# A hybrid attention, convolution and gated-MLP layer: weight sums of four pairs of the up-projection on GpSimd, and another order of the q, k, v chunks

## The chip, the cores and the metric

The kernel runs on one core of a Trainium2 chip. The time is that of the device in microseconds for one execution; a kernel's time is the median of several runs. A core has a matrix engine (TensorE, PE in the profile; its weight loads are PEld), three engines for elementwise work, VectorE (DVE), ScalarE (ACT) and GpSimd (POOL), and SyncE (SP), whose queue issues most of the DMA transfers. Each engine works through its own list of instructions.

## The reference

One layer in float32 over 1024 latent tokens of width 1024 with 256 context tokens ahead of them; batch 1. Cut to what matters:

```python
h  = modulate(x, norm1_w, sh1, sc1)               # RMSNorm, scaled and shifted
q, k, v, hy, gates = split_proj(h @ w_in + b_in)  # q 1024, k 256, v 256 wide, ...
q = apply_rope(rmsnorm(q, q_norm_w)); k = apply_rope(rmsnorm(k, k_norm_w))
attn_o = attend(q, cat(kc, k), cat(vc, v))        # 8 heads of 128, 2 heads of k and v, 1280 keys
hy_o = hyena(hy, ...)                             # long convolution through FFTs
x = x + g1 * merge(attn_o, hy_o, gates, ...)
u = dwconv3(modulate(x, norm2_w, sh2, sc2) @ w_up + b_up, conv_w, conv_b)
a, g = split(u)                                   # 2816 columns each
x = x + g2 * ((gelu(a) * g) @ w_down + b_down)
out = rmsnorm(x, final_norm_w)
```

## The kernel before

Every float32 product is made of three matmuls (lines 184 to 186 issue them): each operand is split into a high part, a rounded copy that ACT casts, and a low part, the difference, that DVE or POOL subtracts (`whi` and `wlo` of a weight block, `PTh` and `PTl` of attention weights).

**q, k and v.** The last part of the projections (lines 996 to 1002) goes over six rounds. In each, one gate chunk (`gate_chunk`, two blocks of columns) is followed by one chunk of 256 columns of q, k or v (`qkv_chunk`): k, v, and four of q. A chunk is projected for eight groups of 128 tokens; what comes behind the matmuls (bias, norm, rotation, transposes, storing) is put on the list `steps` and drained in the following chunk, so that PE has other matmuls meanwhile. A chunk of v only gets its bias and is stored to `v_d`; those of k and q are rotated (`norm_rope`: `ropeA`, `ropeB` on DVE), transposed on PE (`transposed`, tile `tr`) and stored. Beside the first rounds runs the long convolution (`background`).

**Attention.** Sixteen items (loop over `n`), one head and 512 query rows each. For each of ten key blocks, four transposes bring the softmax's weights into a tile `tp` (two buffers), ACT casts `PTh`, DVE subtracts `PTl`, and three matmuls accumulate the output. Scores of the next item are put between. The output of an item is copied to `ou` by ACT, and finished in the next item at key block 7 (`finish`): the reciprocals of the softmax's denominators go out through HBM (`rd_d`) and come back on all partitions as `rb`, POOL multiplies `ou` by it, ACT casts the result (`oTh`), and POOL subtracts `oTl`.

**Sums for the down-projection.** POOL also forms, for eleven items, four sums of blocks of `w_down`: `weights_load` fetches four 256 KB blocks on SP's queue into two tiles `wd` at key block 1, `weight_sums` makes four 128x512 operations at block 7 and stores the results to `ws_d`. The first of them is pinned behind the last operation of `finish`, by `issue_after`, which sets only the order on an engine. Tiles `wd` come from the pool `sgp`, tag "sg" with three buffers.

**Up-projection.** 22 pairs of column blocks, each pair by a scheme of seven products for a 2x2 split. `fetch` loads blocks of `w_up`, `prepare` forms the sums of blocks that products 5, 6, 7 and 3 take (four DVE operations on `wsum` per pair), casts `whi` and returns the subtraction `wlo`. Products of later pairs are put ahead where there is one; in the last four pairs, from `j` = 18, products of the down-projection (8) come between.

The order on each engine is the result of a scheduler, which takes the traced program and its dependences; the code's order is only the start of it.

Of the kernel before, what the change touches and what calls it, by code (L numbers as in the profile page):

```python
# [8 lines left out]
F32 = mybir.dt.float32  # L9
# [6 lines left out]
P = 128  # L16
# [149 lines left out]
def build(tc, A, out, stop=99):  # L166
# [447 lines left out]
    def proj_tok(pool, w, cols, kind, ci, br, qkn, tabs, key0, tok0, nb, bgn=0):  # L614


        ps = pmm.tile([P, 4, 256], F32, name="mm", tag="mm")
        n = len(cols)
        steps = []
        for i, c in enumerate(cols):  # L620
            h, c = c // 512, c % 512
            for k in range(KT):
                mm3(ps[:, i], hTh[h][:, k, c:c + P], hTl[h][:, k, c:c + P], *w[k], k == 0, k == KT - 1)
            if bgn:
                background(bgn)

        def norm_rope(j):
            qr = pool.tile([P, 2, 2, P], F32, name="qr", tag="qr", bufs=nb)
            q3 = qr.rearrange("p t h d -> p t (h d)")
            tt(q3, ps[:, j:j + 2], br.unsqueeze(1).to_broadcast([P, 2, 256]), ALU.add)  # L630
            if kind == "v":
                kt = key0 // P + j
                st(out=v_d[:, kt:kt + 2], in_=q3)
                return None
            ss = stat.tile([P, 4], F32, name="ss", tag="ss4")
            A_ = pool.tile([P, 2, 2, P], F32, name="ropeA", tag="A", bufs=nb)
            for i in range(4):
                S.activation(out=A_[:, i // 2, i % 2], in_=qr[:, i // 2, i % 2], func=AF.Square,
                             accum_out=ss[:, i:i + 1])
            r = rsqrt(ss, 4, HD)  # L640
            q4 = qr.rearrange("p t h d -> p (t h) d")
            for i in range(4):
                S.activation(out=q4[:, i], in_=q4[:, i], func=AF.Copy, scale=r[:, i:i + 1])
            if kind == "kc":
                tt(A_.rearrange("p t h d -> p (t h) d"), q4, qkn[:, 0:1, :].to_broadcast([P, 4, P]), ALU.mult)
            else:
                t0 = tok0 // P + j
                B_ = pool.tile([P, 2, 2, P], F32, name="ropeB", tag="B")
                for o_, tb in ((A_, tabs[0]), (B_, tabs[1])):
                    tt(o_, qr, tb[:, t0:t0 + 2].unsqueeze(2).to_broadcast([P, 2, 2, P]), ALU.mult)  # L650
                sub(A_[..., 0:64], A_[..., 0:64], B_[..., 64:128])
                tt(A_[..., 64:128], A_[..., 64:128], B_[..., 0:64], ALU.add)
            return A_

        def transposed(j, A_):
            tp = ptr.tile([P, 2, 2, P], F32, name="tr", tag="tr")
            for t in range(2):
                for h in range(2):
                    T.transpose(tp[:, h, t], A_[:, t, h], ident)
            t3 = tp.rearrange("p h t d -> p h (t d)")  # L660
            sh = pool.tile([P, 2, 256], F32, name="sth", tag="sth", bufs=nb)
            S.copy(out=sh, in_=t3)
            if kind == "q":
                o = tok0 + j * P
                st(out=qT_d[ci - 2][:, :, o:o + 256].rearrange("h p t -> p h t"), in_=sh)
            else:
                o = key0 + j * P
                st(out=kT_d[:, :, o:o + 256].rearrange("h p t -> p h t"), in_=sh)

        hold = {}  # L670
        for j in range(0, n, 2):
            steps.append(lambda j=j: hold.__setitem__(j, norm_rope(j)))
            if kind != "v":
                steps.append(lambda j=j: transposed(j, hold[j]))
        return steps
# [290 lines left out]
    def gate_chunk(ci, behind=(0, 0)):  # L966
        w = load_w(A["w_in"][12 + ci])
        for m2 in range(2):
            m = 2 * ci + m2
            ps = proj_ch(w, m2, 2)  # L970
            for h in range(2):
                sg = sgpool[0].tile([P, 512], F32, name="sg", tag="sg", bufs=sgpool[1])
                S.activation(out=sg, in_=ps[:, 512 * h:512 * h + 512], func=AF.Identity, bias=bcol(12 + m))  # L973
                (ld if ci > 6 else st)(out=sg_d[m, :, 512 * h:512 * h + 512], in_=sg)
            drain()
            for _ in range(behind[m2]):
                item.score()
# [17 lines left out]

    background(4)
    tabs = rope_tables(1)
    for ci in range(6):
        gate_chunk(ci)
        if ci == 2:  # L1000
            tabs = rope_tables(0)
        qkv_chunk(ci, tabs)
    drain()
# [100 lines left out]

    KH = NJ // 2
    ws_d = tc.dram_tile([4, KH, P, 512], F32, name="ws_d")

    wds = []

    def weights_load(k):  # L1110

        wds[:] = [sgp.tile([P, 2, 512], F32, name="wd", tag="sg") for _ in range(2)]
        for i, (n_, k_) in enumerate(((0, k), (1, k), (1, KH + k), (0, KH + k))):
            ld(out=wds[i // 2][:, i % 2], in_=A["w_down"][n_, k_])

    def weight_sums(k, after):

        t1, t3, t2, t4 = (wds[i // 2][:, i % 2] for i in range(4))
        with tc.issue_after(after.ins):
            sub(t1, t3, t1, G)  # L1120
        sub(t3, t2, t3, G)
        sub(t2, t2, t1, G)
        sub(t4, t4, t2, G)
        for n_, t_ in enumerate((t1, t2, t3, t4)):
            ld(out=ws_d[n_, k], in_=t_)

    late = None
    for n in range(16):
        cur, g = item.Pt, item.h // 4
        nxt = None  # L1130
        if n < 15:
            if (n + 1) % 2 == 0:
                q = load_q((n + 1) // 2, sgp.tile([P, L], F32, name="qf", tag="th", bufs=2))
            nxt = Item(n + 1, q)
        o_ps = pO.tile([P, 512], F32, name="o", tag="o")
        pend = []

        def av(kt, th, tl):
            mm3(o_ps, vv[0][:, kt, g * P:g * P + P], vv[1][:, kt, g * P:g * P + P], th, tl, kt == 0, kt == 9)

        for kt in range(10):
            tp = pT.tile([P, 512], F32, name="tp", tag="tp")
            for i in range(4):
                T.transpose(tp[:, i * P:i * P + P], cur[i][:, kt * P:kt * P + P], ident)  # L1144
            th = ap2.tile([P, 512], F32R, name="PTh", tag="PTh", bufs=4)
            S.copy(out=th, in_=tp)  # L1146
            tl = ap2.tile([P, 512], F32R, name="PTl", tag="PTl", bufs=4)
            sub(tl, tp, th)
            pend.append((kt, th, tl))
            if len(pend) > 2:  # L1150
                av(*pend.pop(0))
            if kt in (1, 3, 5, 7) and nxt:
                nxt.score()
            if kt == 1 and 1 <= n <= KH:
                weights_load(n - 1)
            if kt == 7 and late:
                last_ = finish(*late)
                if n <= KH:
                    weight_sums(n - 1, last_)
        while pend:  # L1160
            av(*pend.pop(0))
        ou = ap2.tile([P, 512], F32, name="ou", tag="ou", bufs=2)
        S.copy(out=ou, in_=o_ps)
        late = (n, ou)
        item = nxt
        if n == 12:
            zts = [z_load(*i) for i in ZT[:3]]
            raw_hy = sgp.tile([P, 2, 2, 256], F32, name="raw_hy", tag="th", bufs=2)
            ld(out=raw_hy, in_=A["w_hy"][0].rearrange("i p (k c) -> p i k c", k=2))
# [295 lines left out]
    def fetch(p, j):  # L1465
        if p == 9 or p == 8 and j < 4:
            raws[p, j] = half_block(act_d[0, j]), half_block(A["w_down"][0, j])
        for b_ in {1: (A11,), 2: (A12,), 6: (A21, A22, A11), 3: (A12,)}.get(p, ()):
            raws[p, j, b_] = half_block(A["w_up"][j, b_])

    def prepare(p, j):
# [3 lines left out]
        if p >= 8:  # L1475
# [13 lines left out]
                for d, src in zip(parts_, r_):  # L1489
                    sub(d[1], src, d[0])  # L1490
            return lows
        if p == 6:
            r21, r22, r11 = (raws[6, j, b_] for b_ in (A21, A22, A11))
            s1, s2, s3 = new(), new(), new()
            tt(s1, r21, r22, ALU.add)
            sub(s2, s1, r11)
            sub(s3, r11, r21)
            sums_[j] = s1, s2, s3
            src = s2
        elif p == 7:  # L1500
            src = sums_[j][2]
        elif p == 5:
            src = sums_[j][0]
        elif p == 4:
            src = raws.pop((6, j, A22))
        elif p == 3:
            src = new()
            sub(src, raws.pop((3, j, A12)), sums_.pop(j)[1])
        else:
            src = raws.pop((p, j, A11 if p == 1 else A12))  # L1510
# [124 lines left out]
    n_ = 0  # L1635
# [238 lines left out]
```

## Time and profile before

| | |
|---|---|
| median of 3 runs | 2023.29 us (2020.77 to 2024.64) |
| profiled execution, its span, its mean granted clock | 2025.56 us, 2023.8 us, 0.975 |
| busy: PE, PEld, DVE, ACT, POOL | 94%, 78%, 76%, 48%, 21% |
| chain that ended last, largest shares | PE 57%, DVE 21%, DMA 6%, issue 5% |
| POOL's sums `wd` and `ou`, `oTl` | 44, 16, 16 operations of 1.29 us |

The busy share of an engine is a mean over stages; a stage is read by its windows, and the waits by the timelines, where `[x <-E tile]` says that the engine stood idle for x us until engine E had done that tile.

### The profile page before, as it was taken

To read this page: it belongs to the slowest core of one execution; us is meant where nothing else is said; L and a number is where in the kernel's file an instruction comes from. 1 tells how busy PE (TensorE), PEld (TensorE's weight loads), DVE (VectorE), ACT (ScalarE), POOL (GpSimd) and SP (SyncE) were. 2 spreads that over 40 slices of the span, in tenths; PEclk is the share of its full clock that TensorE was granted. 3 is DMA by queue.
4 is the path that set the end of the run, shared out by engine and by line. 5 is a ranking of instruction groups with operands and counts; after the bars stand their busy time and mean duration, and the time that the engine had idled before them with its cause. 6 is when DMAs were issued, how large, how long until landed. Compare 5 with 4: busy or idle time off the path is not lost.

```text
span 2023.8 us, 27726 instructions
## 1 busy us (share of the span) xinstructions
PE 1893.8 (94%) x9776; PEld 1570.5 (78%) x9776; DVE 1545.9 (76%) x2630; ACT 968.2 (48%) x1958; POOL 422.0 (21%) x270
## 2 busy tenths in 40 slices
PE   7789899889989989999999999998999999899997
PEld 1667778879878888788887777787888888678885
DVE  6987885896878633677776663889888888878788
ACT  3754443442444334687777332345444444445443
POOL 0553331222141231344532133440000000000000
PEclk8899999999999999999999999999999999999998
DMA  7435434747555331444434874742333333349762
GB/s 296 158 102 201 150 97 156 243 145 240 185 168 158 126 130 58 135 141 150 128 100 85 287 273 168 253 151 65 120 108 106 115 104 109 126 149 339 249 204 98
DMA packets 181131, 322.54 MB, mean 159 GB/s; under 512 B 26955, under 2 KB 65359, under 8 KB 180096
## 3 DMA queue, kind: packets, MB, share of 16 engines
q1 hardware_dynamic: 156256, 287.01, 43.7%
q10 hardware_dynamic: 24736, 33.76, 4.7%
q8 instruction: 77, 1.26, 0.3%
q14 instruction: 62, 0.51, 0.1%
HBM read 245.03 MB, written 75.68 MB: 158 GB/s over the span
## 4 chain that ended last, share of the span: by engine, by line
PE 57%; DVE 21%; DMA 6%; issue 5%; ACT 3%; POOL 2%; SPq 0%; ACTq 0%; DVEq 0%; POOLq 0%
PE mm L186 6%; PE mm L185 6%; PE mm L184 6%; PE b L184 5%; PE b L186 5%; PE b L185 5%; PE tp L1144 3%; DVE ua L180 2%; DVE ug L180 2%; PE s L184 2%; PE s L186 2%; PE s L185 2%; PE o L185 2%; PE o L186 2%; PE o L184 2%
## 5 line engine op out<-in xcount | busy, mean ns | idle before, releaser
L174 POOL TENSOR_TENSOR wlo<-raw,whi 128x512 fp32r<-128x512 f32 x138 | 234.2, 1709 | 601.1 <-ACT whi L497 499.1
L184 PE MATMUL mm<-hTh,whi 128*128 128x512 f32 x448 | 180.5, 403 | 2.6 <-ACT sg L973 1.4
L185 PE MATMUL mm<-hTl,whi 128*128 128x512 f32 x448 | 179.8, 401 | 0.5 <-DVE hTl L174 0.5
L186 PE MATMUL mm<-hTh,wlo 128*128 128x512 f32 x448 | 179.4, 400 | 0.0
L1046 DVE TENSOR_REDUCE mx<-s 128x1 f32<-128x512 f32 (+1 forms) x192 | 113.3, 598 | 58.7 <-PE s L186 57.0
L185 PE MATMUL mm<-wlo,hTh 128*128 128x256 f32 x416 | 118.8, 286 | 8.8 <-POOL wlo L174 8.4
L1051 ACT ACTIVATE Pt<-s,mx 128x512 f32<-128x512 f32 (+1 forms) x192 | 116.1, 614 | 20.2 <-DVE mx L1049 18.8
L186 PE MATMUL mm<-whi,hTl 128*128 128x256 f32 x416 | 118.6, 285 | 0.7 <-DVE hTl L174 0.5
L174 DVE TENSOR_TENSOR PTl<-tp,PTh 128x512 fp32r<-128x512 f32 x160 | 108.2, 685 | 13.7 <-ACT PTh L1146 10.3
L184 PE MATMUL mm<-whi,hTh 128*128 128x256 f32 x416 | 118.5, 285 | 0.0
L388 ACT CAST Xh<-X 128x512 fp32r<-128x512 f32 x128 | 78.0, 620 | 76.1 <-DVE X L177 35.6
L1146 ACT CAST PTh<-tp 128x512 fp32r<-128x512 f32 x160 | 92.7, 594 | 39.5 <-PE tp L1144 39.4
L186 PE MATMUL b<-bh,al 128*128 128x512 f32 x284 | 110.6, 390 | 0.6 <-DVE al L174 0.6
L184 PE MATMUL b<-bh,ah 128*128 128x512 f32 x284 | 110.6, 390 | 0.4 <-ACT ah L1731 0.4
L185 PE MATMUL b<-bl,ah 128*128 128x512 f32 x284 | 110.6, 389 | 0.0
L497 ACT CAST whi<-raw 128x512 fp32r<-128x512 f32 x110 | 66.5, 617 | 87.7 <-PE mm L185 41.2
L174 DVE TENSOR_TENSOR Xl<-X,Xh 128x512 fp32r<-128x512 f32 x112 | 80.6, 737 | 35.2 <-ACT Xh L388 35.0
L184 PEld LDWEIGHTS mm<-hTh,whi 128*128 128x128 f32 x448 | 85.9, 192 | 18.5 <-ACT sg L973 1.8
L186 PEld LDWEIGHTS mm<-hTh,wlo 128*128 128x128 f32 x448 | 86.2, 192 | 16.3
L185 PEld LDWEIGHTS mm<-hTl,whi 128*128 128x128 f32 x448 | 86.3, 193 | 16.0 <-DVE hTl L174 0.9
L1144 PEld LDWEIGHTS tp<-ident,Pt 128*128 128x128 f32 x640 | 77.3, 140 | 22.7 <-issue 3.7
L1144 PE MATMUL tp<-ident,Pt 128*128 128x128 f32 x640 | 93.8, 273 | 1.1 <-DVE PTl L174 0.8
(388 smaller groups left out, 5770.4 us busy)
## 6 DMA issues: line engine op xcount, KB each, us to landing
raw<-w_up SPq DMA_DIRECT2D x132, 256.0 KB, 2.8
raw<-w_in SPq DMA_DIRECT2D x88, 256.0 KB, 3.1
wm<-w_mod SPq DMA_DIRECT2D x64, 256.0 KB, 4.3
raw<-act_d SPq DMA_DIRECT2D x25, 512.0 KB, 3.3
wd<-w_down SPq DMA_DIRECT2D x44, 256.0 KB, 4.2
ws_d<-wd SPq DMA_DIRECT2D x44, 256.0 KB, 4.4
act_d<-ug SPq DMA_DIRECT2D x44, 256.0 KB, 2.2
ft<-fwd_d SPq DMA_DIRECT2D x28, 384.0 KB, 4.0
```

Source lines behind the costliest of these rows:

```text
L174: eng.tensor_tensor(out=out, in0=a, in1=b, op=ALU.subtract)
L180: eng.scalar_tensor_tensor(out=out, in0=a, scalar=s, in1=b, op0=op0, op1=op1)
L184: T.matmul(o, lh, rh, start=start, stop=False, skip_group_check=more)
L185: T.matmul(o, lh, rl, start=False, stop=False, skip_group_check=more)
L186: last_mm[0] = T.matmul(o, ll, rh, start=False, stop=stop, skip_group_check=more)
L388: S.copy(out=h, in_=X)
L497: S.copy(out=hi, in_=raw)
L1046: V.tensor_reduce(out=mx[:, j:j + 1], in_=s[:, :n], axis=AX.X, op=ALU.max)
L1051: S.activation(out=Pt[:, o:o + n], in_=sps[j][:, :n], func=AF.Exp, bias=mx[:, 3:4], accum_out=sm[:, j:j + 1])
L1144: T.transpose(tp[:, i * P:i * P + P], cur[i][:, kt * P:kt * P + P], ident)
L1146: S.copy(out=th, in_=tp)
```

## The change

There are four edits.

- In `transposed` the transposes of rotated groups are issued behind the last matmul that was traced before them.
- The chunks come in the order k, four of q, v; the gate chunks keep their order and q's rotation tables are loaded a round earlier.
- For the last four pairs of the up-projection (`j` = 18 to 21) GpSimd forms the four sums s1 to s4 of blocks of `w_up` during the attention, in items 2, 4, 6 and 8: `up_load` at key block 1 fetches four blocks on SP's queue into two tiles `ud`, one of tag "sg" and one of tag "th" (which it shares with `qf`, the load of the next q); `up_sums` makes four operations and stores the results to `us_d`.
- In these four pairs `fetch` loads the finished sums from `us_d` for products 5, 6, 7 and 3, and the block A22 for product 4, and `prepare` forms no sums.

```diff
--- before.py
+++ after.py
@@ -654,9 +654,10 @@
 
         def transposed(j, A_):
             tp = ptr.tile([P, 2, 2, P], F32, name="tr", tag="tr")
-            for t in range(2):
-                for h in range(2):
-                    T.transpose(tp[:, h, t], A_[:, t, h], ident)
+            with tc.issue_after(last_mm[0].ins):
+                for t in range(2):
+                    for h in range(2):
+                        T.transpose(tp[:, h, t], A_[:, t, h], ident)
             t3 = tp.rearrange("p h t d -> p h (t d)")
             sh = pool.tile([P, 2, 256], F32, name="sth", tag="sth", bufs=nb)
             S.copy(out=sh, in_=t3)
@@ -995,9 +996,9 @@
 
     background(4)
     tabs = rope_tables(1)
-    for ci in range(6):
-        gate_chunk(ci)
-        if ci == 2:
+    for i, ci in enumerate((0, 2, 3, 4, 5, 1)):
+        gate_chunk(i)
+        if i == 1:
             tabs = rope_tables(0)
         qkv_chunk(ci, tabs)
     drain()
@@ -1104,6 +1105,8 @@
 
     KH = NJ // 2
     ws_d = tc.dram_tile([4, KH, P, 512], F32, name="ws_d")
+    us_d = tc.dram_tile([4, 4, P, 512], F32, name="us_d")
+    J0 = NJ - 4
 
     wds = []
 
@@ -1123,6 +1126,24 @@
         sub(t4, t4, t2, G)
         for n_, t_ in enumerate((t1, t2, t3, t4)):
             ld(out=ws_d[n_, k], in_=t_)
+
+    uds = []
+
+    def up_load(j):
+
+        uds[:] = [sgp.tile([P, 2, 512], F32, name="ud", tag=t_, bufs=n_) for t_, n_ in (("sg", 3), ("th", 2))]
+        for i, b_ in enumerate((2, 1, 0, 3)):
+            ld(out=uds[i // 2][:, i % 2], in_=A["w_up"][j, b_])
+
+    def up_sums(j):
+
+        s1, s3, s2, s4 = (uds[i // 2][:, i % 2] for i in range(4))
+        tt(s1, s1, s3, ALU.add, G)
+        sub(s3, s2, s3, G)
+        sub(s2, s1, s2, G)
+        sub(s4, s4, s2, G)
+        for n_, t_ in enumerate((s1, s2, s3, s4)):
+            ld(out=us_d[j - J0, n_], in_=t_)
 
     late = None
     for n in range(16):
@@ -1153,10 +1174,14 @@
                 nxt.score()
             if kt == 1 and 1 <= n <= KH:
                 weights_load(n - 1)
+                if n in (2, 4, 6, 8):
+                    up_load(J0 + n // 2 - 1)
             if kt == 7 and late:
                 last_ = finish(*late)
                 if n <= KH:
                     weight_sums(n - 1, last_)
+                    if n in (2, 4, 6, 8):
+                        up_sums(J0 + n // 2 - 1)
         while pend:
             av(*pend.pop(0))
         ou = ap2.tile([P, 512], F32, name="ou", tag="ou", bufs=2)
@@ -1465,6 +1490,9 @@
     def fetch(p, j):
         if p == 9 or p == 8 and j < 4:
             raws[p, j] = half_block(act_d[0, j]), half_block(A["w_down"][0, j])
+        if j >= J0 and p in (3, 4, 5, 6, 7):
+            raws[p, j] = half_block(A["w_up"][j, A22] if p == 4 else us_d[j - J0, {5: 0, 6: 1, 7: 2, 3: 3}[p]])
+            return
         for b_ in {1: (A11,), 2: (A12,), 6: (A21, A22, A11), 3: (A12,)}.get(p, ()):
             raws[p, j, b_] = half_block(A["w_up"][j, b_])
 
@@ -1489,7 +1517,9 @@
                 for d, src in zip(parts_, r_):
                     sub(d[1], src, d[0])
             return lows
-        if p == 6:
+        if j >= J0 and p in (3, 4, 5, 6, 7):
+            src = raws.pop((p, j))
+        elif p == 6:
             r21, r22, r11 = (raws[6, j, b_] for b_ in (A21, A22, A11))
             s1, s2, s3 = new(), new(), new()
             tt(s1, r21, r22, ALU.add)
```

The order on POOL around item 2 of the attention was, before (`ou` normalised, `oTl` its low part, `wd` the sums of `w_down`, `qT` the low part of the next q):

```order
L1096 TENSOR_TENSOR oTl<-ou,oTh 128x512
L174 TENSOR_TENSOR wd<-wd 128x512 x4
L177 TENSOR_TENSOR ou<-ou,rb 128x512
L1096 TENSOR_TENSOR oTl<-ou,oTh 128x512
L174 TENSOR_TENSOR wd<-wd 128x512 x4
L174 TENSOR_TENSOR qT<-qf,qT 128x1024
```

and is now, with `ud` the sums of `w_up`:

```order
L1097 TENSOR_TENSOR oTl<-ou,oTh 128x512
L174 TENSOR_TENSOR wd<-wd 128x512 x4
L177 TENSOR_TENSOR ud<-ud 128x512
L174 TENSOR_TENSOR ud<-ud 128x512 x3
L177 TENSOR_TENSOR ou<-ou,rb 128x512
L1097 TENSOR_TENSOR oTl<-ou,oTh 128x512
L174 TENSOR_TENSOR wd<-wd 128x512 x4
L174 TENSOR_TENSOR qT<-qf,qT 128x1024
```

The four `ud` sums stand ahead of the next `ou`, and not behind its `oTl`; the same occurs in items 4, 6 and 8.

On SP's queue the same stretch was, before, from one `rb` (the load for an `ou`) on:

```order
L1093 DMA rb<-rd_d 128x512
L1125 DMA ws_d<-wd 128x512 x4
L1114 DMA wd<-w_down 128x512 x4
L1071 DMA rd_d<-rc 128x4x1
L1093 DMA rb<-rd_d 128x512
L1125 DMA ws_d<-wd 128x512 x4
L1114 DMA wd<-w_down 128x512 x4
```

and is now:

```order
L1128 DMA ws_d<-wd 128x512 x4
L1117 DMA wd<-w_down 128x512 x2
L1136 DMA ud<-w_up 128x512 x2
L1146 DMA us_d<-ud 128x512 x4
L1117 DMA wd<-w_down 128x512 x2
L1018 DMA qf<-qT_d_58 128x1024
L1072 DMA rd_d<-rc 128x4x1
L1128 DMA ws_d<-wd 128x512 x4
L1094 DMA rb<-rd_d 128x512
```

Two of the four places of `wd` loads are taken by `ud` loads (the other two `ud` loads were issued ahead of the `rd_d` before this piece); the stores `us_d`, the other `wd` loads and the next `qf` now stand ahead of `rd_d`, and `ws_d` ahead of `rb`.

On DVE, in pair 18 of the up-projection, from the `wlo` ahead of the first `u` to the second `u`, there was:

```order
L174 TENSOR_TENSOR wlo<-raw,whi 128x512
L174 TENSOR_TENSOR wsum<-raw,wsum 128x512
L177 TENSOR_TENSOR u_17539<-c_16926,b 128x512
L174 TENSOR_TENSOR m0l<-raw,m0h 128x512 x4
L174 TENSOR_TENSOR wlo<-wsum,whi 128x512
L180 SCALAR_TENSOR_TENSOR ua<-ca,vecs,ua 128x1023 x2
L177 TENSOR_TENSOR ua<-ua,edge_ff 128x2
L177 TENSOR_TENSOR wsum<-raw 128x512
L174 TENSOR_TENSOR wsum<-wsum,raw 128x512
L174 TENSOR_TENSOR wsum<-raw 128x512
L177 TENSOR_TENSOR u_17574<-u_17539,b 128x512
```

and there is now:

```order
L174 TENSOR_TENSOR wlo<-raw,whi 128x512
L177 TENSOR_TENSOR u_17588<-c_16983,b 128x512
L174 TENSOR_TENSOR m0l<-raw,m0h 128x512 x4
L174 TENSOR_TENSOR wlo<-raw,whi 128x512
L180 SCALAR_TENSOR_TENSOR ua<-ca,vecs,ua 128x1023 x2
L177 TENSOR_TENSOR ua<-ua,edge_ff 128x2
L177 TENSOR_TENSOR u_17619<-u_17588,b 128x512
```

The four `wsum` are gone, and the rest keeps its order.

## Rows read from the trace of the kernel before

**Rows 1.** The page, part 1: engine, busy us, share of the span, instructions
```profile
PE 1893.8 (94%) x9776; PEld 1570.5 (78%) x9776; DVE 1545.9 (76%) x2630; ACT 968.2 (48%) x1958; POOL 422.0 (21%) x270
```

**Rows 2.** 20-us stretches: PE, PEld, DVE, ACT, POOL busy (count), PE clock, DMA, GB/s
```profile
840.00:860.00 20.00, 20.00 (x118) 16.77 (x117) 15.81 (x36) 14.81 (x39) 9.44 (x8) 1.00 0.40 119
1720.00:1740.00 20.00, 20.00 (x89) 16.54 (x89) 15.23 (x22) 9.19 (x14) 0.00 (x0) 1.00 0.33 106
```

**Rows 3.** Timeline of POOL: start, us, line, operation, [idle before <-releaser], attention
```profile
839.52 5.41 POOL L174 TENSOR_TENSOR wd<-wd 128x512 f32<-128x512 f32 x4
...
854.45 1.30 POOL L177 TENSOR_TENSOR ou<-ou,rb 128x512 f32<-128x512 f32 x1 [9.52 <-ACT ou L1163]
...
891.30 1.29 POOL L177 TENSOR_TENSOR ou<-ou,rb 128x512 f32<-128x512 f32 x1 [9.57 <-ACT ou L1163]
...
928.15 1.30 POOL L177 TENSOR_TENSOR ou<-ou,rb 128x512 f32<-128x512 f32 x1 [9.58 <-ACT ou L1163]
...
964.98 1.29 POOL L177 TENSOR_TENSOR ou<-ou,rb 128x512 f32<-128x512 f32 x1 [9.55 <-ACT ou L1163]
```

**Rows 4.** Timeline of SP's queue: issues of the `wd` loads before these four
```profile
850.78 1.76 SPq L1114 DMA_DIRECT2D wd<-w_down  x4
...
889.45 1.81 SPq L1114 DMA_DIRECT2D wd<-w_down  x4
...
925.72 2.44 SPq L1114 DMA_DIRECT2D wd<-w_down  x4
...
961.68 1.76 SPq L1114 DMA_DIRECT2D wd<-w_down  x4
```

**Rows 5.** The tile `wd`: durations in ns min/median/max, and landing
```profile
L174 POOL TENSOR_TENSOR wd<-wd x44: 1279/1291/1312, 839.5 to 1027.8; 128x512 f32<-128x512 f32 x44
DMA to landing us min/median/max: 2.9/4.4/6.6
```

**Rows 6.** Timeline of ACT behind the normalisation at 854.45
```profile
855.78 0.62 ACT L1095 CAST oTh<-ou 128x512 fp32r<-128x512 f32 x1 [0.43 <-POOL ou L177]
856.76 0.59 ACT L1146 CAST PTh<-tp 128x512 fp32r<-128x512 f32 x1 [0.36 <-PE tp L1144]
```

**Rows 7.** Timeline of PE, third group of transposes behind it
```profile
859.39 0.60 PE L1144 MATMUL tp<-ident,Pt 128*128 128x128 f32 x4
```

**Rows 8.** Timeline of DVE, the low part that frees the buffer
```profile
857.61 0.68 DVE L174 TENSOR_TENSOR PTl<-tp,PTh 128x512 fp32r<-128x512 f32 x1
```

**Rows 9.** Timeline of PE at the start of the attention
```profile
819.63 0.49 PE L184 MATMUL o<-PTh,v 128*128 128x512 f32 x1 [2.92 <-ACT PTh L1146]
```

**Rows 10.** Timeline of PE in the last four pairs
```profile
1749.49 0.77 PE L184 MATMUL b<-T4h,whi 128*128 128x512 f32 x1 [7.69 <-DVE u L177]
...
1753.79 0.39 PE L185 MATMUL b<-T4l,whi 128*128 128x512 f32 x1
```

**Rows 11.** Line 1071, the issue of `rd_d`: time to landing
```profile
DMA to landing us min/median/max: 7.9/8.1/8.4
```

**Rows 12.** Timeline of DVE in the last four pairs, before the stall's end
```profile
1739.80 0.69 DVE L174 TENSOR_TENSOR wsum<-raw,wsum 128x512 f32<-128x512 f32 x1 [2.64 <-DMA raw<-w_up]
...
1744.01 2.60 DVE L180 SCALAR_TENSOR_TENSOR ua<-ca,vecs,ua 128x1023 f32<-128x1023 f32 x2
...
1748.66 0.68 DVE L177 TENSOR_TENSOR u<-u,b 128x512 f32<-128x512 f32 x1
```

**Rows 13.** Timeline of PE in the last chunk of q
```profile
758.65 1.09 PE L659 MATMUL tr<-ident,ropeA 128*128 128x128 f32 x4 [5.42 <-DVE ropeA L177]
```

**Rows 14.** Stretches of 20 us in the long convolution
```profile
440.00:460.00 20.00, 19.72 (x140) 18.16 (x139) 20.00 (x51) 14.48 (x41) 10.82 (x4) 1.00 0.82 245
480.00:500.00 20.00, 20.00 (x136) 18.51 (x135) 9.51 (x15) 5.66 (x10) 5.10 (x4) 1.00 0.77 256
```

**Rows 15.** Timeline of ACT, the cast of `v`
```profile
740.34 1.26 ACT L1018 CAST v<-Pt 128x1280 fp32r<-128x1280 f32 x1 [9.52 <-DMA Pt<-v_d]
```

**Rows 16.** Timeline of POOL in the projections
```profile
586.70 14.61 POOL L174 TENSOR_TENSOR wlo<-raw,whi 128x512 fp32r<-128x512 f32 x2 [18.91 <-ACT whi L497]
```

## The prediction

> **What bounds the kernel now.** I read the page first: TensorE (PE) is busy 94% of the span [rows 1], so a change pays only where PE stands still. The table by stretches says where that is not the case: in the attention and in the up-projection PE is busy for 20.00 us of 20 at full clock, while GpSimd (POOL) works 9.44 us of 20 in the attention and nothing in the up-projection [rows 2]. POOL has room; the question is what stands behind its new work. The timeline of POOL shows the rhythm of the attention: the normalisation `ou` of an item, its low part `oTl`, the four sums `wd`, then idle until the next `ou`; the four `ou` that matter here came after 9.5 us of idling [rows 3]. The timeline of SyncE's queue (SP) shows that the loads of `wd` are issued only some 1 to 4 us before those same `ou` [rows 4].
>
> **Part 1, the sums of w_up on GpSimd.** The order puts each new group of four `ud` sums behind the old `wd` sums and ahead of the next `ou`, in four of the sixteen items. GpSimd goes in order, so `ou` waits for the sums and these for their loads. The first sum needs the `ud` tile whose two loads now stand where the third and fourth `wd` load stood in SP's queue. Terms, one item each:
> - Sums: one 128x512 sum on POOL takes 1291 ns, and a transfer of such a block 4.4 us from issue to landing, 2.9 to 6.6 [rows 5]. I take 4.2 us for a load (about the median) and 4 x 1.29 = 5.2, with the rows' own 5.41 for four [rows 3] = 5.4 us.
> - Second item: four loads in 1.76 us from 850.78, the last issued at about 852.1 [rows 4]; landed at 856.3, sums done at 861.7, where `ou` stood at 854.45 [rows 3]: 7.2 us late.
> - Fourth: last issue 889.45 + 1.81 - 0.43 = 890.8, landed 895.0, done 900.4 against 891.30: 9.1 late. Sixth: 925.72 + 2.44 - 0.43 = 927.7, then 937.3 against 928.15: 9.2 late. Eighth: 963.0, then 972.6 against 964.98: 7.6 late. Together 33.1 us.
> - What PE feels: ScalarE's (ACT) cast `oTh` waits for `ou`, and in ACT's order the casts `PTh` of the attention weights stand behind it [rows 6]. PE still has scores and two products queued until the transposes of 859.39, the first that need a buffer of `tp` back [rows 7]. That buffer is free after cast `PTh` (0.59 us) and the subtraction `PTl` on VectorE (DVE), 0.68 us [rows 8]; counted from the `ou` of before this would have been at about 857.7, so 1.7 us of each delay are swallowed. 33.1 - 4 x 1.7 = 26.3 us of standing.
> - That such a chain reaches PE is seen at the attention's start, where PE stood for 2.92 us because ACT's `PTh` came late [rows 9].
> - The clock. After the stall of 7.69 us before 1749.49 ten 512-column matmuls took 4.30 us up to 1753.79 [rows 10]; at full clock 89 matmuls take 20 us [rows 2], so ten take 2.25, and the slow level (1.2 GHz of 2.4) cost 2.05 us. The four new stalls are 5.5 to 7.5 us long, so up to 4 x 2.05 = 8.2; below, zero, if they leave the clock as it is. I take 6.
> - The four stores `us_d` and the loads of the other half add 32 transfers to SP's queue. Behind the stores stands `rd_d`, the denominators' way through HBM, that takes 8.1 us to land [rows 11], and then `rb`, the load that the next `ou` needs. With the sums done at 861.7, `rd_d` goes out about 865, lands at 873, and `rb` 4.4 us later, at 877.4; the next `ou` stood at 873 and is 5.5 us later now. That is 1 us to spare, so nothing, and up to 2 us per item if not: 8 us, for the upper end.
>
> Sum: +32 us (bounds 0 and +42).
>
> By the Trainium skill, page "DMA: Bandwidth & Descriptors", section "Anatomy of one DMA — SWDGE (gpsimd) path", a transfer costs about 2.0 us and its bytes at 436 GB/s, thus an estimate of 2.6 us for 256 KB. The rows say 4.4, with 2.9 as the least [rows 5], and the measurement decides; by the page the loads would land 1.6 us sooner and the part would be 4 x 1.6 = 6.4 us cheaper, still a loss.
>
> **Part 2, the up-projection.** DVE loses four `wsum` operations in each of the last four pairs. PE is full there before and after, except at one place: the 7.69 us stall [rows 10], whose releaser is DVE's `u` of 1748.66. In the chain ahead of it, DVE idled 2.64 us for a block of `w_up`, made one `wsum` (0.60 to the next start), and after `ua` (ending at 1746.61) three more until 1748.66, 2.05 us with a small edge operation [rows 12]. Without all of that `u` comes up to 5.2 us sooner, but the operations ahead of it then wait for PE's own products and ACT's casts, so I take 4. A stall of some 3.7 us still lowers the clock for a while; 0.5 of the 2.05 comes back. So -4.5, bounds -9.7 (stall and clock both gone) and 0 (the extra block loaded per pair is late instead). The other 12 `wsum` lie beside a full PE and are worth nothing.
>
> **Part 3, the chunks of q, k, v.** With v last there are no rotated transposes in the last chunk. The stall of 5.42 us before 758.65, where PE waited for DVE's `ropeA`, goes [rows 13], and with it a slow stretch priced as above: -7.4. What comes back: the rotation of the first q chunk moves into the long convolution, around 440 to 500 us, where DVE is busy 20.00 of 20 us in one slice and 9.51 in another [rows 14]; that is four rotations, each of three 128x512 operations and two of half the columns, so at 0.60 us from start to start [rows 12] about 2.4 us each and 10 in all (an estimate; some short operations come on top). And `v` is now stored just before it is read back: ACT's cast of `v` already waited 9.52 us for that load [rows 15], and the last two gate weight blocks are cast behind it. I put 5 on the two together, between 0 and 11. So -2.4, bounds -7.4 and +3.6. Pinning the transposes issues them behind a matmul of PE's own queue; it adds no wait and the other q chunks keep their places: 0.
>
> One row speaks for more: two `wlo` on POOL that took 14.61 us where a sum takes 1.29 [rows 16, 5]. The Trainium skill, page "SBUF — State Buffer", section "SBUF: two separate sides", has a rule for it: DVE and GpSimd share a port pair as an exclusive lock, and a DVE operation with two SBUF inputs locks a GpSimd operation that reads SBUF out. Rotations are such operations. By this rule the moved rotations would hold up POOL's `wlo` in the convolution; the third rival prices this from the row.
>
> **Sum.** +32 - 4.5 - 2.4 = +25, on the profiled execution's 2025.6: 2050.7. That execution is 2.3 us above the median of the three runs, so about 2048 as a median.
>
> **The rivals.**
> 1. The sums don't reach PE: faster. If the `ud` loads land before the last `wd` sums are through, or the delays stay under the 1.7 us that are swallowed, part 1 is 0 and parts 2 and 3 stand: 2023.3 - 6.9 = about 2016. For it: POOL idles 9.5 us ahead of each of these `ou` [rows 3], and four sums need 5.4. Against it: that idling lies before the loads land. It decides from a landing at or before 850.7 (854.45 + 1.7 - 5.4), and the loads were issued at 850.78 and later. Only if the new queue issues these loads some 4 us sooner does this happen.
> 2. The loss is half: ACT and PE find more slack than the 1.7 us (PE's score work runs ahead), or the loads land at the lower end of 2.9 us, and the clock stays up: 33.1 - 4 x (1.3 + 3) = 16, less 6.9: about 2032.
> 3. The moved rotations hold up POOL's `wlo` in the convolution, and PE waits for these: two of them took 14.61 us there instead of 2 x 1.29, so one more such case is +12 us on top of the +5 taken: about 2060. For it that row, against it the slice in which DVE works 9.51 us only.
> 4. No effect: the losses of part 1 are swallowed to about 7 us and balance the gains, 2023.
>
> **How the numbers follow.** Forecast with its own range 2038 to 2058: 0.54. Rival 1: 0.12, rival 2: 0.20, rival 3: 0.08, rival 4: 0.06. A measurement of this kernel can tell about 0.2%, 4 us, so same means 2019 to 2027. Faster is rival 1 with little else, 0.12; same is rival 4 and the lower edge of rival 2, 0.08; slower 0.80. The range for 8 times in 10 leaves out rival 1, most of 4 and the far half of 3: 2024 to 2060.
>
> **What would show it.** In the changed profile POOL's `ou` of the second, fourth, sixth and eighth item must start directly behind four `ud` sums, and PE must have four gaps of 4 to 8 us, released by ACT's `PTh` or DVE's `PTl`, between 855 and 1000 us, with the granted clock below 1.00 behind them. If these gaps are missing, part 1 is wrong, and the forecast with it. The gap at 758 should be gone, the one at 1742 shorter by about 4 us. If the total is over 2060, the place to look is the stretch of 440 to 600, or `rb` landing behind `ou`.

## The result, and the profile after

The changed kernel took 2045.63 us (median, 2043.07 to 2047.22), the kernel before 2022.99 us beside it: ratio 1.0109, 95% interval 1.0096 to 1.0121. It is slower by 22 us; 2048 had been forecast. The profiled executions stand 21.6 us apart in their spans (2045.4 and 2023.8), and that difference can be followed along the program.

The page, part 1 of the changed kernel, answers to [rows 1]: PE has 4 us more of work and a longer span, POOL 16 operations more.

```profile
PE 1898.1 (93%) x9776; PEld 1573.8 (77%) x9776; DVE 1534.6 (75%) x2614; ACT 966.1 (47%) x1958; POOL 437.5 (21%) x286
```

**Attention.** The timeline of POOL in the changed kernel (start, length, operation, idle before and releaser; answers to [rows 3]):

```profile
852.74 1.28 POOL L177 TENSOR_TENSOR ud<-ud 128x512 f32<-128x512 f32 x1 [11.60 <-DMA ud<-w_up]
854.11 3.97 POOL L174 TENSOR_TENSOR ud<-ud 128x512 f32<-128x512 f32 x3
858.04 1.26 POOL L177 TENSOR_TENSOR ou<-ou,rb 128x512 f32<-128x512 f32 x1
...
897.84 1.28 POOL L177 TENSOR_TENSOR ud<-ud 128x512 f32<-128x512 f32 x1 [12.01 <-DMA ud<-w_up]
...
903.13 1.26 POOL L177 TENSOR_TENSOR ou<-ou,rb 128x512 f32<-128x512 f32 x1
...
943.74 1.29 POOL L177 TENSOR_TENSOR ud<-ud 128x512 f32<-128x512 f32 x1 [13.12 <-DMA ud<-w_up]
...
949.01 1.26 POOL L177 TENSOR_TENSOR ou<-ou,rb 128x512 f32<-128x512 f32 x1
...
968.83 1.30 POOL L177 TENSOR_TENSOR ou<-ou,rb 128x512 f32<-128x512 f32 x1 [1.59 <-DMA rb<-rd_d]
...
989.72 1.29 POOL L177 TENSOR_TENSOR ud<-ud 128x512 f32<-128x512 f32 x1 [12.21 <-DMA ud<-w_up]
...
995.00 1.26 POOL L177 TENSOR_TENSOR ou<-ou,rb 128x512 f32<-128x512 f32 x1
```

The idle time that stood ahead of `ou` [rows 3] now stands ahead of the `ud` sums, longer than before and released by their loads, and `ou` follows the sums without a pause. SP's queue shows the loads at the place of [rows 4], and behind them the stores, `rd_d` and `rb`:

```profile
848.25 0.85 SPq L1136 DMA_DIRECT2D ud<-w_up  x2
854.05 4.37 SPq L1146 DMA_DIRECT2D us_d<-ud  x4
...
860.62 0.57 SPq L1072 DMA_DIRECT2D rd_d<-rc  x1
862.55 4.39 SPq L1128 DMA_DIRECT2D ws_d<-wd  x4
871.47 0.32 SPq L1094 DMA_DIRECT2D rb<-rd_d  x1
```

ACT, in its order, held the casts `PTh` behind `oTh` (answers to [rows 6]), and PE stood at the transposes, as at 859.39 before [rows 7]. ACT first, then the four gaps of PE in the attention:

```profile
850.00 0.60 ACT L1188 COPY ou<-o 128x512 f32<-128x512 f32 x1
...
859.33 0.62 ACT L1096 CAST oTh<-ou 128x512 fp32r<-128x512 f32 x1 [7.76 <-POOL ou L177]
859.86 1.06 ACT L1167 CAST PTh<-tp 128x512 fp32r<-128x512 f32 x2
```

```profile
861.21 1.12 PE L1165 MATMUL tp<-ident,Pt 128*128 128x128 f32 x4 [5.42 <-DVE mx L1049]
...
906.30 1.11 PE L1165 MATMUL tp<-ident,Pt 128*128 128x128 f32 x4 [5.85 <-DVE mx L1049]
...
952.19 1.11 PE L1165 MATMUL tp<-ident,Pt 128*128 128x128 f32 x4 [6.89 <-DVE mx L1049]
...
998.18 1.12 PE L1165 MATMUL tp<-ident,Pt 128*128 128x128 f32 x4 [6.09 <-DVE mx L1049]
```

The releaser named is the last thing DVE had done; the transposes also wait for the buffer of `tp` that DVE's `PTl` frees, and that stood idle 6.55 us for ACT's `PTh`:

```profile
860.47 0.69 DVE L174 TENSOR_TENSOR PTl<-tp,PTh 128x512 fp32r<-128x512 f32 x1 [6.55 <-ACT PTh L1167]
```

The four gaps are 24.25 us. The stretches of 20 us of the changed kernel (columns as in [rows 2]) show the clock behind them:

```profile
860.00:880.00 20.00, 18.79 (x96) 15.51 (x97) 14.09 (x32) 15.33 (x38) 10.85 (x8) 0.85 0.88 195
...
900.00:920.00 20.00, 14.15 (x69) 11.29 (x68) 11.01 (x25) 11.95 (x31) 12.49 (x10) 0.83 0.87 167
...
940.00:960.00 20.00, 13.11 (x61) 10.46 (x59) 8.61 (x20) 7.45 (x20) 12.61 (x10) 0.74 0.73 166
...
980.00:1000.00 20.00, 13.91 (x75) 11.20 (x74) 9.50 (x22) 9.00 (x24) 9.24 (x8) 0.89 0.64 216
```

From the first output matmul behind the gap at the start of the attention to the first matmul of the Hyena output behind it, the changed kernel took 1138.63 - 815.84 = 322.8 us; the kernel before from 819.63 [rows 9] to 1108.41, 288.8 us. So the stretch cost 34.0 us, 24.25 as gaps and 9.8 as slow work. The stretch as a whole says the same: the same 1646 matmuls kept PE busy for 296.10 us in place of 286.21, at a mean granted clock of 0.95 in place of 1.00. After, then before:

```profile
815.84 0.50 PE L184 MATMUL o<-PTh,v 128*128 128x512 f32 x1 [2.66 <-ACT PTh L1167]
...
1138.63 0.74 PE L184 MATMUL mm<-hyh,whi 128*128 128x512 f32 x2 [1.16 <-ACT hyh L1254]
```

```profile
815.84:1138.63 322.79, 296.10 (x1646) 243.94 (x1646) 220.06 (x486) 224.73 (x564) 136.34 (x101) 0.95 0.53 132
```

```profile
1108.41 0.98 PE L184 MATMUL mm<-hyh,whi 128*128 128x512 f32 x3 [1.16 <-ACT hyh L1229]
```

```profile
819.63:1108.41 288.78, 286.21 (x1646) 237.79 (x1646) 220.30 (x486) 226.00 (x564) 116.51 (x85) 1.00 0.43 119
```

**Projections.** The attention starts 3.8 us sooner (815.84 against 819.63). The gap at 758 [rows 13] is gone; rotated transposes now stand in PE's way in the convolution, for 4.43 and 2.20 us, while two other waits that PE had there before, of 3.10 us (520.06) and 1.45 us (528.99), are gone. ACT waits 16.74 us for `v` in place of 9.52 [rows 15], and PE has no gap there. PE, then ACT:

```profile
523.71 0.63 PE L660 MATMUL tr<-ident,ropeA 128*128 128x128 f32 x4 [4.43 <-DVE ropeA L177]
...
566.43 0.66 PE L660 MATMUL tr<-ident,ropeA 128*128 128x128 f32 x4 [2.20 <-DVE ropeA L177]
```

```profile
754.21 1.26 ACT L1019 CAST v<-Pt 128x1280 fp32r<-128x1280 f32 x1 [16.74 <-DMA Pt<-v_d]
```

**Up-projection.** The stall of 7.69 us [rows 10] is 1.75 us long, and the first ten matmuls behind it take 2.37 us (1773.86 to 1776.23), at full clock, where they took 4.30. On DVE only a wait of 1.05 us for PE took the place of the `wsum` and their load [rows 12]. PE, then DVE, then the DVE line of before that answers to 1766.71:

```profile
1773.86 0.47 PE L184 MATMUL b<-T4h,whi 128*128 128x512 f32 x1 [1.75 <-DVE u L177]
...
1776.23 0.39 PE L185 MATMUL b<-T4l,whi 128*128 128x512 f32 x1
```

```profile
1766.71 0.69 DVE L177 TENSOR_TENSOR u<-c,b 128x512 f32<-128x512 f32 x1 [1.05 <-PE b L186]
...
1770.33 2.60 DVE L180 SCALAR_TENSOR_TENSOR ua<-ca,vecs,ua 128x1023 f32<-128x1023 f32 x2
...
1773.03 0.68 DVE L177 TENSOR_TENSOR u<-u,b 128x512 f32<-128x512 f32 x1
```

```profile
1740.40 0.68 DVE L177 TENSOR_TENSOR u<-c,b 128x512 f32<-128x512 f32 x1
```

The ledger by the spans: -3.8 before the attention, +34.0 in it, 0.1 from there to the stall, -5.9 the stall, -2.8 behind it (about 2 of it the clock): +21.6.

### The profile page after: what moved, and what is told of

It is laid out like the page before. It is cut to its first block, busy times and chain, and to the rows that moved or that the text cites. A ratio compares the mean times of both kernels' runs of the same rounds, so it can differ in the third digit from the quotient of the medians.

```text
span 2045.4 us, 27787 instructions
## 1 busy us (share of the span) xinstructions
PE 1898.1 (93%) x9776; PEld 1573.8 (77%) x9776; DVE 1534.6 (75%) x2614; ACT 966.1 (47%) x1958; POOL 437.5 (21%) x286
## 4 chain that ended last, share of the span: by engine, by line
PE 65%; DVE 12%; DMA 8%; POOL 4%; issue 3%; ACT 2%; SPq 1%; DVEq 0%; ACTq 0%; POOLq 0%
PE b L184 9%; PE b L186 9%; PE b L185 9%; PE mm L185 6%; PE mm L186 6%; PE mm L184 6%; PE tp L1165 2%; DMA wm<-w_mod 2%; POOL wlo L174 1%; DMA rd_d<-rc 1%; PE s L184 1%; PE s L185 1%; PE s L186 1%; PE o L185 1%; PE o L186 1%
```

## The experiments

The kernel before was run beside each group; its medians on the three later occasions were 2025.4, 2029.3 and 2029.3 us, so only ratios to it are compared.

**1. The chunks alone, with the pinned transposes.**

```diff
-    for ci in range(6):
-        gate_chunk(ci)
+    for i, ci in enumerate((0, 2, 3, 4, 5, 1)):
+        gate_chunk(i)
```

> Only the order of the chunks and the pinned transposes; w_up is summed on VectorE as before. Theory (each part pays by itself): the attention begins 3.8 us sooner, as in the changed kernel (816.7 against 813.2 at the end of its first scores), nothing else moves, total about 2019 us. Rival (the gain at the chunks is only a shift that the attention's start swallows): no change, 2023 us. PE's gap at 758 is gone in both; a new one by rotated transposes near 519 of 4.4 us in both.

Ratio 0.9981 (0.9970 to 0.9992), 4 us faster: the theory's figure. The stall of the last pairs stayed (7.64 us).

**2. The sums alone**, the changed kernel with the loop and `transposed` of before.

```diff
-    for i, ci in enumerate((0, 2, 3, 4, 5, 1)):
+    for ci in range(6):
```

> Only the sums of w_up on GpSimd and what reads them; chunks and transposes as before. Theory: the whole loss is here, four PE gaps of 5.4 to 6.9 us in the attention and a slow clock behind each, +34 us, and -8.4 us at the stall of the last four pairs: about 2049 us, slower than the changed kernel by 3.8. Rival (the chunks' new order makes the attention's loads late): the gaps shrink to under 3 us each, total under 2035 us.

Ratio 1.0134 (1.0114 to 1.0154), 27 us slower, as expected: the loss is the sums' alone. Its four gaps were 4.42, 5.72, 5.88 and 6.97 us, so they don't come from the chunks.

**3. The sums left out, the transfers kept.**

```diff
-        tt(s1, s1, s3, ALU.add, G)
-        sub(s3, s2, s3, G)
-        sub(s2, s1, s2, G)
-        sub(s4, s4, s2, G)
```

> The changed kernel without the four additions of w_up blocks on GpSimd: the blocks are loaded and stored as they are, so the products of the last four pairs take unsummed weights. All transfers stay. Theory (GpSimd goes in order, and the normalisation stands behind sums that wait for late loads): nothing stands ahead of the normalisation, the four gaps are gone, 2045.6 - 34 = about 2011 us. Rival (SyncE's queue: 32 more transfers make the denominators' way and the load rb late): the gaps stay at half their length or more, total over 2025 us.

Ratio 1.0043 (1.0027 to 1.0059): the theory's 2011 us was missed, and three gaps of 6.05, 4.07 and 4.84 us remained; the one of item 2 was gone. (They are read from the fastest of its eleven executions, 2026.69 us; the median is 2034.2.) These gaps have another cause. POOL's `ou` was now held by `rb`:

```profile
846.24 1.30 POOL L177 TENSOR_TENSOR ou<-ou,rb 128x512 f32<-128x512 f32 x1 [9.49 <-ACT ou L1184]
...
891.04 1.26 POOL L177 TENSOR_TENSOR ou<-ou,rb 128x512 f32<-128x512 f32 x1 [17.53 <-DMA rb<-rd_d]
```

On SP's queue, in front of that `rb`, a store `us_d` now waits for its own load's landing, and `rd_d` stands behind it: the reciprocals were ready at 864.70, and `rd_d` went out at 873.33.

```profile
868.02 0.90 SPq L1136 DMA_DIRECT2D ud<-w_up  x2
872.96 0.33 SPq L1142 DMA_DIRECT2D us_d<-ud  x1
873.33 0.43 SPq L1072 DMA_DIRECT2D rd_d<-rc  x1
873.87 0.53 SPq L1142 DMA_DIRECT2D us_d<-ud  x1
874.49 3.08 SPq L1128 DMA_DIRECT2D ws_d<-wd  x4
884.58 0.32 SPq L1094 DMA_DIRECT2D rb<-rd_d  x1
```

So the run changed the queue as well, and does not price GpSimd's part. It shows the second route: a store that waits in SP's queue makes `rd_d`, and so `rb`, late. In the changed kernel that route took 1.59 us ahead of one `ou`, at 968.83.

**4. The sums on GpSimd in the up-projection itself**, for the last four pairs, on top of experiment 1.

```diff
-            tt(s1, r21, r22, ALU.add)
-            sub(s2, s1, r11)
-            sub(s3, r11, r21)
+            e_ = G if j >= NJ - 4 else V
+            tt(s1, r21, r22, ALU.add, e_)
+            sub(s2, s1, r11, e_)
+            sub(s3, r11, r21, e_)
```

(and likewise for product 3)

> The chunks' order and pinned transposes, and GpSimd forms the sums of w_up of the last four pairs in the up-projection itself, where it is idle, from the blocks loaded there; nothing is added to the attention, no us_d. Theory (what helps the last stall is VectorE's freed time, wherever the sums are formed): stall at 1742 down from 7.7 to about 1.8 us, total 2023 - 3.8 - 8.4 = about 2011 us. Rival (a sum takes GpSimd 1.3 us or more beside VectorE, and the casts behind it come late): the stall stays at 5 us or more, total about 2018 us.

Ratio 0.9985 (0.9974 to 0.9997), no better than experiment 1: the rival. The stall was 6.48 us, though DVE had no `wsum`. Beside POOL's sums, four of the first eight of which took 2.0 us or more in place of 1.29 [rows 5], the same operations of DVE were slower: four `m0l` 3.59 us (2.49 in the changed kernel), two `ua` 4.49 (2.60), the edge operation behind them 1.10 (0.16). That is 3.9 us more ahead of the `u` that releases PE, of the 4.7 by which the stall exceeds that of the changed kernel. POOL, then DVE:

```profile
1740.22 2.00 POOL L174 TENSOR_TENSOR wsum<-wsum,raw 128x512 f32<-128x512 f32 x1 [0.21 <-DMA raw<-w_up]
1742.18 2.24 POOL L174 TENSOR_TENSOR wsum<-raw 128x512 f32<-128x512 f32 x1
```

```profile
1734.47 3.59 DVE L174 TENSOR_TENSOR m0l<-raw,m0h 128x512 fp32r<-128x512 f32 x4 [0.48 <-ACT m0h L1487]
...
1738.82 4.49 DVE L180 SCALAR_TENSOR_TENSOR ua<-ca,vecs,ua 128x1023 f32<-128x1023 f32 x2
```

By the Trainium skill, page "SBUF — State Buffer", section "SBUF: two separate sides", a GpSimd operation that reads SBUF and a VectorE operation with two SBUF inputs take the port pair that they share in turn, each for a whole operation. The slow operations here agree with it in kind: all of them have two SBUF inputs. Which of them held the pair when, the trace does not show.

**5. The sums pinned behind the sums of `w_down`.**

```diff
-        tt(s1, s1, s3, ALU.add, G)
+        with tc.issue_after(after.ins):
+            tt(s1, s1, s3, ALU.add, G)
```

(`after` is the fourth sum of `weight_sums`)

> The changed kernel with the four sums of w_up pinned behind the four sums of w_down of the same item, so that the normalisation no longer stands behind them; transfers as before, but the stores of the sums and all that stands behind them on SyncE's queue go out later. Theory (place on GpSimd and place on the queue both count, since the tile shared with qf is freed by these stores): the four gaps released through the normalisation are gone, and new ones come where ScalarE waits for qf, which now goes out some 10 us later than in the changed kernel, up to 10 us each: between 2025 and 2060 us. Rival (only the order on GpSimd counts): 2045.6 - 34, about 2011 us.

Ratio 1.0051 (1.0032 to 1.0069), 10 us slower than before and faster than the changed kernel. The gaps through `ou` are gone, and three others of 3.51, 4.45 and 9.06 us stand where ACT, with `PTh` behind it, waits for `qf`:

```profile
875.25 1.04 ACT L1019 CAST qT<-qf 128x1024 fp32r<-128x1024 f32 x1 [4.32 <-DMA qf<-qT_d]
876.20 1.07 ACT L1169 CAST PTh<-tp 128x512 fp32r<-128x512 f32 x2
...
966.63 1.04 ACT L1019 CAST qT<-qf 128x1024 fp32r<-128x1024 f32 x1 [9.89 <-DMA qf<-qT_d]
```

Each place has its price: the order on GpSimd, and the order on the queue, where `qf` now goes out at 869.98, behind the stores `us_d` (862.11 to 864.96) and six loads of `wd`. That it is the tile shared with `qf` that makes it wait, and not its place on the queue alone, is read from the code; no run separates the two.

**6. Pairs 18 and 19 alone, in items 2 and 4.**

```diff
-                if n in (2, 4, 6, 8):
+                if n in (2, 4):
```

(`fetch` and `prepare` likewise, `J0 <= j < J0 + 2`)

> The changed kernel with the sums on GpSimd for pairs 18 and 19 alone, in items 2 and 4; pairs 20 and 21 keep VectorE's sums. Theory (each item pays its own gap, and only the first two of the last four pairs had a stall to lose): two gaps of 5.4 and 5.9 us instead of four, half of the 34 us, and the stall of the last four pairs as short as in the changed kernel: 2023 - 4 + 17 - 8.4 = about 2028 us. Rival (a common cost of all the transfers): nearer to 2040 us.

Ratio 1.0039 (1.0020 to 1.0057), 8 us slower than before where 5 were expected: two gaps and no more, so there is no common cost of all transfers; but they were 7.08 and 9.66 us long, more than in the changed kernel, since this queue sent the `ud` loads only 6.2 and 3.7 us before PE stopped, where the changed kernel sent them 7.5 and 7.7 us before. The stall of the last pairs was 1.75 us: pairs 18 and 19 are all that it needs.

**7. Pairs 18 and 19 in items 0 and 12**, on top of experiment 1.

```diff
-        uds[:] = [sgp.tile([P, 2, 512], F32, name="ud", tag=t_, bufs=n_) for t_, n_ in (("sg", 3), ("th", 2))]
+        uds[:] = [sgp.tile([P, 2, 512], F32, name="ud", tag=t_, bufs=n_) for t_, n_ in (("sg", 3), ("sg", 3))]
...
+            if kt == 1 and n in {0: 18, 12: 19}:
+                up_load({0: 18, 12: 19}[n])
+            if kt == 7 and n == 0 and n in {0: 18, 12: 19}:
+                up_sums({0: 18, 12: 19}[n])
             if kt == 7 and late:
                 last_ = finish(*late)
+                if n in {0: 18, 12: 19}:
+                    up_sums({0: 18, 12: 19}[n], last_)
```

(the calls in items 2, 4, 6 and 8 go; `fetch` and `prepare` take the finished sums for `j` 18 and 19 alone)

> Chunks and pinned transposes as changed; sums on GpSimd for pairs 18 and 19 alone, formed in item 0, before the first sums of w_down, and in item 12, behind the last of them, there pinned behind the low part of the output; both tiles from the pool of the w_down blocks, none from that of qf. Theory (the cost is one of place, the gain at the last stall needs these two pairs only): no gap in items 2, 4, 6, 8, stall of the last four pairs about 1.8 us, 2023.3 - 4 - 8.4 = about 2011 us. Rival (the added transfers delay rb or qf in any item): gaps of 4 us or more in items 0 to 2 and 12 to 13, about 2020 us.

Ratio 0.9914 (0.9889 to 0.9939): 17 us faster than the kernel before, where 12 were expected, and so faster than the changed kernel too. PE is full between 840 and 940 us, and the stall is 1.75 us.

**8. The chunks' order without the pin**, the loop of experiment 1 with `transposed` of before.

```diff
-            with tc.issue_after(last_mm[0].ins):
```

> Only the chunks' order, without the pinned transposes. Theory (the scheduler puts the moved rotated transposes elsewhere, and the pin is what keeps them from standing early in PE's order): slower than with the pin, by the length of one or two waits for rotations, 2021 to 2028 us. Rival (the pin is without effect): as with both, about 2019 us.

Ratio 0.9976 (0.9962 to 0.9990), not to be told from experiment 1: the pin has no effect that these runs can tell, my expectation of a slowdown was wrong, and the rival holds. The same gaps of 4.44 and 2.20 us stand at 523 and 566.

**9 and 10. The free items with the old chunks, and experiment 7 again.** The ninth is the seventh with the loop and `transposed` of before (the diff of experiment 2).

> The kernel before with one thing added: the sums for pairs 18 and 19 formed on GpSimd in items 0 and 12, chunks and transposes as before. Theory (chunks and sums are worth their parts, 4 and 8.4 us, independently): 8 us faster than the kernel before, ratio 0.996. Rival (the gain of the free items came with the chunks' order, which clears item 0): no faster than the kernel before.

> The same kernel as in the run with free items, chunks as changed, on another occasion. Theory: 12 us faster than the kernel before, ratio 0.994, and 4 us faster than with the old chunks. Rival (its ratio of 0.991 was the occasion's): 0.997 or above.

0.9944 (0.9927 to 0.9960) and 0.9924 (0.9903 to 0.9944): 11 and 15 us faster than before. The sums in free items pay without the chunks' order. The order adds about its 4 us to them, though the two intervals overlap. Part of what is above 8.4 shows at the start of the attention, where the gap of 2.9 us [rows 9] was 1.25; the rest is not settled. The stretches of the tenth run show PE full, at full clock, where the changed kernel had its four gaps:

```profile
840.00:940.00 100.00, 100.00 (x579) 83.59 (x577) 78.22 (x174) 79.37 (x200) 47.27 (x36) 1.00 0.49 143
940.00:1040.00 100.00, 100.00 (x577) 83.35 (x576) 77.67 (x174) 78.11 (x195) 49.15 (x36) 1.00 0.49 145
```

## Why the prediction was right

- **The mechanism of part 1** held at each link: late loads, sums, `ou`, `oTh`, `PTh`, `tp`. Before, `ou` started 0.67 us behind the start of ACT's copy (854.45 against 853.78). Measured from there it was now 7.4, 7.8, 8.8 and 8.0 us late (858.04 - 850.00 - 0.67 and so on), 32.0 in sum where 33.1 were forecast. Of it 7.8 were swallowed (6.8 forecast) and 24.25 felt (26.3).
- **The clock was under-priced:** 9.8 us in place of 6, more than my upper end of 8.2. The price from one gap of 7.69 us, 2.05, was taken as the most; here a gap of 5.4 to 6.9 us cost 2.45 on the mean. The kernel before had a dearer case: behind the shorter stop of 3.94 us before 703.09, twelve 512-column matmuls took 5.27 us (703.82 to 709.09) where full clock makes 2.70 [rows 2]. The errors of gaps and clock have opposite signs: +34.0 against +32.
- **`rb`**, which had 1 us to spare in the working, was late once, by 1.59 us ahead of an `ou`; nothing was taken, and nothing much came.
- **Part 2 was under-sized:** -4.5 forecast, -8.7 measured by the ledger. The step that failed is that the operations ahead of `u` would wait for PE and ACT: they waited 1.05 us. The 5.2 us that it took as the most was too little as well: the stall shrank by 5.94. Before, VectorE reached the first `u` 1.4 us before PE stopped (1740.40, 1741.80); now it waits there for PE, 5.4 us before PE stops (1766.71, 1772.11). That is 4.0 us, and the three `wsum` behind it are the other 1.9. Of the 4.0 the wait for the block and its `wsum` make 3.2; the rest would fit the three earlier `wsum` of pair 18 (1726.92 to 1728.86 before), which the prediction had held to be worth nothing, but no run shows that. The shorter stall also left the clock at full, and all of the 2.05 us came back, of which I had taken 0.5. Of the four `wsum` in the stall one is the last of pair 18 and three are the first of pair 19, by the order in experiment 4, where only pairs from 18 on are summed on POOL. So experiment 6 bears out that the sums of pairs 20 and 21 are worth nothing there.
- **Part 3:** -2.4 forecast, -3.8 by the trace and -4 by experiment 1. The load of `v` cost nothing, though ACT waited 7.2 us longer, and the rotations brought waits of 4.43 and 2.20 us into the convolution, where 4.55 us of others went: 2.1 us came back of the 5 that I had put on the rotations and the load together.
- **Rivals.** The first (sums that don't reach PE) asked for loads that land 3.8 us before `ou` is due (850.7 against 854.45); they landed 2.1 us after it (852.74, where `ou` was due at 850.67). The second, half the loss, asked for gaps of 4 us and a clock that stays up; the least gap was 5.42 us. The third (rotations that hold up POOL's `wlo`) asked for one more such wait of PE: there was one of 8.36 us before (600.12), and one of 8.36 us now (606.98), and no other above 0.9 us. The fourth, no effect, is out by the interval of the ratio.
- **The price of a transfer.** From the last issue to the first sum the `ud` loads of item 2 needed about 4.1 us (852.74 less 848.67), those of the other three items 4.0 to 4.6, near the 4.2 taken. By the Trainium skill, page "DMA: Bandwidth & Descriptors", section "Anatomy of one DMA — SWDGE (gpsimd) path", the estimate was 2.6 us. That section's fit is for transfers issued by GpSimd, and these were issued on SP's queue; the measurement decides.

The forecast of +25 against +22 was thus right in its mechanism, and wrong in the sizes of the clock (too small) and of parts 2 and 3 (too small as gains). These have opposite signs; that the total came so near is in part luck.

## What to carry to other kernels

An idle engine is free only if nothing that it must do next stands behind the new work: read the order on it, and ask when the new work's *loads* land, not how long it takes. Four groups of sums cost 34 us ahead of an operation on the chain; two of them, in items 0 and 12 with both tiles from the pool of the `w_down` blocks, left PE without a gap of that kind. And move only the work that a stall waits for: with two of the four pairs the stall was as short as with all (1.75 us).

## What the runs showed of the hardware that was not expected

- GpSimd's sums and VectorE's operations on SBUF slowed each other: sums up to 2.26 us in place of 1.29, and `ua` 4.49 us for two in place of 2.60 (experiment 4).
- A short stop, 1.75 us, left the matmuls behind it at full clock; the four stops of 5.4 to 6.9 us did not: their next 512-column matmuls stood 0.43 us apart in place of 0.23, for 4 us and more. The same spacing stood behind shorter stops, of 3.94 us (before, at 703.09) and 3.51 us (experiment 5, at 877.56).
- `rd_d`, 8.1 us to land before [rows 11], took 9.9 in the median of the changed kernel, where the DMA engines were busy for 0.53 of the attention's stretch in place of 0.43; that the one comes from the other is not shown:

```profile
DMA to landing us min/median/max: 8.2/9.9/11.7
```
